# Four one-bank accumulators for a depthwise convolution, and its first two tiles of the larger group ahead of the first layer norm

## The chip, the core and the metric

The kernel runs on one core of a Trainium2 chip. Its engines are called PE (TensorE, matrix products; PEld is the loading of weights into it), DVE (VectorE), ACT (ScalarE), POOL (GpSimd) and SP (SyncE, which issues most DMAs here). Each engine works through its own queue in order and waits on semaphores for the others. The metric is the device time of one execution in microseconds (us).

## The reference, cut to what matters

One step of a streaming encoder, for one new stream of 512 frames and 8 running streams of 16 new frames each, D = 1024. Layer 0 is a convolution module and a feed-forward network (FFN); layer 1 is attention in bands of chunks, and an FFN. The change lies in layer 0's convolution module:

```python
def conv_module(h, hist, g, w_pw1, b_pw1, w_dw, b_dw, ln_g, ln_b, w_pw2, b_pw2):
    a, gate = jnp.split(rms_norm(h, g) @ w_pw1 + b_pw1, 2, axis=-1)
    glu = a * jax.nn.sigmoid(gate)
    full = jnp.concatenate([hist.astype(glu.dtype), glu], axis=1)
    y = lax.conv_general_dilated(
        full, w_dw[:, None, :].astype(full.dtype), window_strides=(1,), padding="VALID",
        dimension_numbers=("NWC", "WIO", "NWC"), feature_group_count=D_MODEL) + b_dw
    y = jax.nn.silu(layer_norm(y, ln_g, ln_b))
    return h + y @ w_pw2 + b_pw2, full[:, -CONV_HIST:]

def swiglu_ffn(h, g, w_in, w_out):
    a, b = jnp.split(rms_norm(h, g) @ w_in, 2, axis=-1)
    return h + (jax.nn.silu(a) * b) @ w_out
```

The depthwise convolution has 31 taps, so each of the 1024 channels is 31 multiply-adds along time. Everything is float32.

## The kernel before, in words

Features lie on the partitions, 8 channel tiles of 128, and the 640 frames on the columns, in two groups. The small group (g = 0) has 256 columns: the 128 frames of the running streams and the first 128 of the prompt. The larger group (g = 1) has the other 384 columns of the prompt.

A float32 product is made of three matmuls (`mm3`, L170 to L172): high part of the weight times high part of the data, low times high, high times low. So each weight is split after its load (`wsplit`, L128): ACT copies it to the high part (L150), and the low part is raw minus high (L154), of which DVE does the first columns and POOL the rest. For the FFN chunks of the small group, DVE does 512 of 2048 columns and POOL 1536 (384 and 1152 of 1536 for the output weights). A matmul of L171 needs the low part, so PE waits there for the slower of the two.

The steps of layer 0:

- pw1 and GLU, one channel tile at a time: products on PE, tanh and bias on ACT (L380, L383), the product of the two halves on DVE (L386 into `gs` for the small group, L395 into `gp` for the larger).
- the convolution, in three ways by channel tile. On DVE (`conv`, L420): per tap a multiply-add into an accumulator in PSUM (L434 the first tap, L437 the other 30), several tiles interleaved tap by tap; at the end ACT copies the sum to `y` (L440). On PE (`conv_pe`, with its staging through DRAM). On ACT and POOL (`conv_pool`): ACT multiplies, POOL adds into `y` (L417).
- the layer norm over the channels (`conv_ln`): POOL adds tiles of `y` (L195), PE sums over the partitions (L204), DVE collects (L208), PE spreads the mean (L216), DVE subtracts (L483); ACT squares (L179), POOL adds, PE sums, DVE and POOL make the root (L226, L230), DVE multiplies (L489), ACT applies the swish, and the result is split into high and low parts.
- pw2 (`pw2`), whose results DVE adds to `h` (L506), then the FFN. Its hidden tiles are worked in chunks of six. The first three chunks are done for the small group alone (chunk one, two and three here), each with six input weights and four output weights (output sums: L303); PE does them while DVE, ACT and POOL convolve for the larger group. Then pw2 of the larger group follows, and the other chunks for both groups.

The order in which the program is written out is the string `PLAN`, one token a step: `a`, `b` pw1 and GLU of a tile for the small and the larger group; `d` the convolution on DVE of one group (first digit) for the listed tiles, so `d0213` is the small group's tiles 2, 1 and 3, and `d101`, `d145`, `d127` are the larger group's tiles 0 and 1, 4 and 5, 2 and 7; `l` and `p` load and run the convolution on PE; `q` is the one on ACT and POOL; `n` the layer norm, `w` pw2, `r` the norm ahead of the FFN, `f` one chunk of the FFN, `s` the store of the convolution's history. A scheduler then orders each engine's queue by its own model of times, with higher priority for the weight splits and the GLU; the pools of buffers limit what can run ahead.

The accumulators come from the PSUM pool `w2`, which also serves the norms:

```python
w2 = w2s.enter_context(tc.tile_pool(name="w2", bufs=2, space=PSUM))
...
sts = [w2t() for _ in range(0, len(cs), 2)]
sts = [sts[i // 2][:, i % 2 * 512:i % 2 * 512 + n] for i in range(len(cs))]
```

It has two buffers of 1024 columns, that is two banks each. Two channel tiles share a buffer, one bank each.

## Time and profile before

| | |
|---|---|
| median of 3 runs | 1550.37 us (1547.32 to 1551.12) |
| the profiled run | 1551.3 us, of which the span is 1549.5 |
| instructions in the span | 26569 |
| mean granted PE clock | 0.984 |
| PE busy | 1471.7 us, 95% |
| DVE busy | 1050.1 us, 68% |
| ACT, POOL busy | 662.4 us (43%), 443.8 us (29%) |

The profile is of one execution. Its page gives the busy time of each engine over the span and over 40 equal slices (each digit is the busy share in tenths), and groups of instructions by source line: engine, operation, output and inputs by the program's names, shape, count, then busy time and the mean ns of one, then the idle time ahead of them. A timeline row gives start, duration, the instruction, and in brackets how long the engine had been idle and what ended that.

### The profile page before, as it was taken

What the parts mean: (1) busy time and instruction counts of PE and PEld (TensorE: products, weight loads), DVE (VectorE), ACT (ScalarE), POOL (GpSimd) and SP (SyncE); (2) the same over time, 40 slices, a digit from 0 to 9 for tenths busy, and PEclk for the clock granted to TensorE, in tenths of its full rate; (3) what the DMA queues carried; (4) which work ended last, traced back from release to release, by engine and by line L of the source; (5) the groups of instructions that cost most, each with busy time, mean ns of one, the idle gap of its engine ahead of it and who ended that gap; (6) DMA issues with size and microseconds to landing.
All of it is one profiled execution on the core that took longest, in us unless ns stands there. A gap on an engine that the chain in (4) does not pass through costs nothing.

```text
span 1549.5 us, 26569 instructions
## 1 busy us (share of the span) xinstructions
PE 1471.7 (95%) x10770; PEld 1398.9 (90%) x10770; DVE 1050.1 (68%) x1863; ACT 662.4 (43%) x1173; POOL 443.8 (29%) x403
## 2 busy tenths in 40 slices
PE   5888998989999999999999999999989999999997
PEld 5878888989999999999988798886989999999997
DVE  6994999988555455457576767566796476476455
ACT  4544454535423323235454445443554244244244
POOL 6865568877501000001321211110411121121110
PEclk9999999999999999999999999998999999999998
DMA  7784434444421333433655545453103213213211
GB/s 236 234 228 142 137 113 159 148 157 153 147 82 55 129 116 129 135 118 126 202 183 201 174 140 205 133 175 114 55 28 109 82 56 109 82 55 109 82 55 68
DMA packets 59658, 199.95 MB, mean 129 GB/s; under 512 B 10128, under 2 KB 22672, under 8 KB 46736
## 3 DMA queue, kind: packets, MB, share of 16 engines
q1 hardware_dynamic: 59248, 197.96, 39.1%
q8 instruction: 84, 1.38, 0.4%
q10 hardware_dynamic: 288, 0.31, 0.1%
q14 instruction: 38, 0.31, 0.1%
HBM read 187.02 MB, written 11.22 MB: 128 GB/s over the span
## 4 chain that ended last, share of the span: by engine, by line
PE 71%; DVE 16%; ACT 3%; issue 3%; DMA 3%; POOL 2%; SPq 0%; POOLq 0%; DVEq 0%; ACTq 0%
PE mm L170 12%; PE mm L172 12%; PE mm L171 12%; PE pb L968 6%; DVE w L437 5%; DVE wlo L154 4%; PE pc L968 4%; PE pa L968 4%; PE pb L170 1%; PE pb L171 1%; PE pb L172 1%; PE pa L172 1%; PE pa L170 1%; PE pc L170 1%; PE pc L172 1%
## 5 line engine op out<-in xcount | busy, mean ns | idle before, releaser
L171 PE MATMUL mm<-x,wlo 128*128 128x256 f32 (+1 forms) x1344 | 416.8, 312 | 15.4 <-DVE wlo L154 14.9
L170 PE MATMUL mm<-x,whi 128*128 128x256 f32 (+1 forms) x1344 | 413.3, 312 | 6.4 <-ACT x L159 3.7
L172 PE MATMUL mm<-x,whi 128*128 128x256 f32 (+1 forms) x1344 | 412.7, 311 | 0.5
L150 ACT ACTIVATE whi<-raw 128x2048 fp32r<-128x2048 f32 (+2 forms) x117 | 197.7, 1694 | 232.6 <-PE mm L172 138.8
L171 PEld LDWEIGHTS mm<-x,wlo 128*128 128x128 f32 x1344 | 257.1, 192 | 18.7 <-DVE wlo L154 17.5
L170 PEld LDWEIGHTS mm<-x,whi 128*128 128x128 f32 x1344 | 254.5, 191 | 11.2 <-ACT x L159 4.1
L172 PEld LDWEIGHTS mm<-x,whi 128*128 128x128 f32 x1344 | 255.1, 191 | 2.9 <-DVE x L160 1.8
L154 DVE TENSOR_TENSOR wlo<-raw,whi 128x2048 fp32r<-128x2048 f32 (+5 forms) x117 | 214.0, 1832 | 62.2 <-ACT whi L150 61.2
L154 POOL TENSOR_TENSOR wlo<-raw,whi 128x1536 fp32r<-128x1536 f32 (+3 forms) x50 | 145.7, 2918 | 69.0 <-ACT whi L150 69.0
L913 POOL TENSOR_TENSOR raw<-raw 128x512 f32<-128x512 f32 x38 | 50.5, 1330 | 332.3 <-DVE raw L913 257.5
L171 PE MATMUL mm<-hid,wlo 128*128 128x256 f32 (+1 forms) x352 | 107.7, 308 | 6.6 <-DVE wlo L154 6.6
L172 PE MATMUL mm<-hid,whi 128*128 128x256 f32 (+1 forms) x352 | 105.8, 307 | 0.2
L170 PE MATMUL mm<-hid,whi 128*128 128x256 f32 (+1 forms) x352 | 104.6, 307 | 0.1
L437 DVE SCALAR_TENSOR_TENSOR w<-gp,dwv,w 128x384 f32<-128x384 f32 x180 | 103.9, 612 | 0.8
L195 POOL TENSOR_TENSOR acc<-sq,sq 128x384 f32<-128x384 f32 (+1 forms) x8 | 8.1, 1006 | 258.2 <-ACT sq L179 258.1
L171 PEld LDWEIGHTS mm<-hid,wlo 128*128 128x128 f32 x352 | 66.0, 188 | 7.8 <-DVE wlo L154 7.8
L417 POOL TENSOR_TENSOR y<-y,cvt 128x256 f32<-128x256 f32 (+1 forms) x60 | 69.3, 1154 | 6.3 <-ACT cvt L416 4.0
L172 PEld LDWEIGHTS mm<-hid,whi 128*128 128x128 f32 x352 | 65.7, 188 | 0.6 <-DVE hid L160 0.6
L159 ACT ACTIVATE whi<-raw 128x1024 fp32r<-128x1024 f32 x38 | 39.4, 1054 | 61.6 <-PE pc L172 18.1
L170 PEld LDWEIGHTS mm<-hid,whi 128*128 128x128 f32 x352 | 65.2, 188 | 0.4 <-ACT hid L159 0.3
L968 PE MATMUL pa<-x0f,whi 128*128 128x320 f32 x228 | 61.2, 316 | 2.5 <-DVE t L913 2.3
L195 POOL TENSOR_TENSOR acc<-acc,sq 128x384 f32<-128x384 f32 (+1 forms) x48 | 52.7, 1097 | 28.9 <-ACT sq L179 27.5
(317 smaller groups left out, 3391.4 us busy)
## 6 DMA issues: line engine op xcount, KB each, us to landing
raw<-in_w_in SPq DMA_DIRECT2D x62, 1024.0 KB
raw<-in_w_out SPq DMA_DIRECT2D x36, 768.0 KB
raw<-in_w_pw SPq DMA_DIRECT2D x22, 1024.0 KB
cache<-in_ck SPq DMA_DIRECT2D x32, 512.0 KB
cache<-in_cv SPq DMA_DIRECT2D x32, 512.0 KB
raw<-in_w_kq SPq DMA_DIRECT2D x8, 1024.0 KB
x<-sc SPq DMA_DIRECT2D x16, 368.0 KB
raw<-in_w_out SPq DMA_DIRECT2D x4, 1024.0 KB
```

The source lines that it names most:

```text
L150: nc.scalar.activation(out=hi[:, a:b], in_=raw[:, a:b], func=AF.Copy)
L154: eng.tensor_tensor(out=lo[:, a:b], in0=raw[:, a:b], in1=hi[:, a:b].bitcast(F32), op=ALU.subtract)
L159: nc.scalar.activation(out=hi, in_=src, func=AF.Copy)
L170: nc.tensor.matmul(ps, wh, xh, start=(i == 0), stop=False)
L171: nc.tensor.matmul(ps, wl, xh, start=False, stop=False)
L172: nc.tensor.matmul(ps, wh, xl, start=False, stop=(i == last))
L195: last["acc"] = eng.tensor_tensor(out=acc[:, :n], in0=prev, in1=s(), op=ALU.add)
L417: nc.gpsimd.tensor_tensor(out=y[g][:, c, :], in0=y[g][:, c, :], in1=pr[:, :n], op=ALU.add)
L437: nc.vector.scalar_tensor_tensor(out=dst, in0=src, scalar=wj, in1=dst, op0=ALU.mult, op1=ALU.add)
L913: ENG[e].tensor_tensor(out=out, in0=a, in1=b, op=op)
L968: nc.tensor.matmul(ps, a[:, c], b[:, k, :], start=(first and k == 0 and i == 0), stop=(k == 3 and i == 2), skip_group_check=not first)
```

## The change

Four things, which belong together:

- The pool `w2` has four buffers of 512 columns (one bank) instead of two of 1024, and each channel tile of a convolution on DVE has a buffer of its own. The norm's sums move from column 512 to column 384 of their buffer, into the same bank as the spread mean. Before the attention the pool is closed and one of two buffers of 1024 columns opened, as the attention had it before.
- A convolution's first instructions are issued only behind the last instruction of the convolution ahead of it (`after(last.get("conv"))`).
- In `PLAN`, `d101` moves from behind `q16 s1` to just ahead of `n0`, the small group's layer norm.
- The layer norm `conv_ln` is written with high priority.

```diff
-PLAN = ("a0 y a1 a2 a4 x a3 a5 a6 l04 p04 l05 d0213 a7 b0 p05 b1 l07 p07 l06 b2 q00 s0 p06 n0 b3 b4 b5 d145 l13 w0 b7 r0 p13 b6 f q16 s1 d101 d127 n1 f f w1 r1")
+PLAN = ("a0 y a1 a2 a4 x a3 a5 a6 l04 p04 l05 d0213 a7 b0 p05 b1 l07 p07 l06 b2 q00 s0 p06 d101 n0 b3 b4 b5 d145 l13 w0 b7 r0 p13 b6 f q16 s1 d127 n1 f f w1 r1")
...
-    w2 = w2s.enter_context(tc.tile_pool(name="w2", bufs=2, space=PSUM))
+    w2 = w2s.enter_context(tc.tile_pool(name="w2", bufs=4, space=PSUM))
...
-    sums = [512]
+    wide_w2 = [512]
...
-        return w2.tile([P, 1024 if sums[0] == 512 else 512], F32, tag="w2", name=nm("w2"))
+        return w2.tile([P, wide_w2[0]], F32, tag="w2", name=nm("w2"))
...
+    def after(ins):
+        return tc.issue_after(ins.ins) if ins is not None else ExitStack()
...
-        w, c0 = len(srcs), sums[0]
+        w, c0 = len(srcs), 384
...
-        sts = [w2t() for _ in range(0, len(cs), 2)]
-        sts = [sts[i // 2][:, i % 2 * 512:i % 2 * 512 + n] for i in range(len(cs))]
+        sts = [w2t()[:, 0:n] for _ in cs]
...
                 if j == 0:
-                    nc.vector.tensor_scalar(out=dst, in0=src, scalar1=wj, scalar2=col(V_BDW, c),
-                                            op0=ALU.mult, op1=ALU.add)
+                    with after(last.get("conv")):
+                        nc.vector.tensor_scalar(out=dst, in0=src, scalar1=wj,
+                                                scalar2=col(V_BDW, c), op0=ALU.mult,
+                                                op1=ALU.add)
...
+        last["conv"] = end
...
-            zs[g] = conv_ln(g)
+            with tc.high_priority(offset=HP):
+                zs[g] = conv_ln(g)
...
+    w2s.close()
...
+    w2 = aps.enter_context(tc.tile_pool(name="w2a", bufs=2, space=PSUM))
+    wide_w2[0] = 1024
```

What this does to the queues, at three places. The rows are instructions in the order of one engine's queue: line, operation, output, inputs, shape, and a count where one repeats. The lines of the changed kernel stand 3 to 5 further down from the middle of the file on (L437 is L441, L483 is L488, L303 is L306).

First, DVE's queue in the small group's layer norm, before: from the sum's collection (L208) to the root (L226). `gp` is the GLU of the larger group, `wlo` a low part of a weight, `y` the convolved tile, `w_213` an accumulator.

```order
L208 TENSOR_REDUCE mst_1357<-w_168_1345 128x2
L480 COPY mst_1357<-mst_1357 128x2
L154 TENSOR_TENSOR wlo_1569<-raw_1567,whi_1568 128x2048
L483 TENSOR_TENSOR y_106<-y_106,w_168_1345 128x256 x8
L395 SCALAR_TENSOR_TENSOR gp<-t_204_1562,t_205_1564 128x384
L154 TENSOR_TENSOR wlo_1704<-raw_1702,whi_1703 128x1024
L434 TENSOR_SCALAR w_213_1628<-gp,dwv,vec 128x384
L226 TENSOR_SCALAR rst_1397<-w_171_1370 128x2
```

The same place after; `w_169` and `w_170` are the accumulators of `d101`.

```order
L211 TENSOR_REDUCE mst_1424<-w_171_1412 128x2
L441 SCALAR_TENSOR_TENSOR w_170_1347<-gp,dwv,w_170_1347 128x384
L441 SCALAR_TENSOR_TENSOR w_169_1346<-gp,dwv,w_169_1346 128x384
L485 COPY mst_1424<-mst_1424 128x2
L441 SCALAR_TENSOR_TENSOR w_170_1347<-gp,dwv,w_170_1347 128x384
L398 SCALAR_TENSOR_TENSOR gp<-t_200_1568,t_201_1570 128x384
L441 SCALAR_TENSOR_TENSOR w_169_1346<-gp,dwv,w_169_1346 128x384
L441 SCALAR_TENSOR_TENSOR w_170_1347<-gp,dwv,w_170_1347 128x384
L154 TENSOR_TENSOR wlo_1636<-raw_1634,whi_1635 128x2048
```

All 62 instructions of `d101` now stand between the small group's convolution and the norm's later steps; before, all of them stood behind that norm.

Second, DVE's queue at the end of chunk one. Before, the convolution (`w_366`, `w_367`, tiles of `d127` and `d101`) goes on past the last weight split of chunk one (`wlo_2683`), and past the first of chunk two:

```order
L154 TENSOR_TENSOR wlo_2683<-raw_2681,whi_2682 128x384
L437 SCALAR_TENSOR_TENSOR w_366_2820<-gp,dwv,w_366_2820 128x384
L437 SCALAR_TENSOR_TENSOR w_367_2885<-gp,dwv,w_367_2885 128x384
L303 TENSOR_TENSOR h<-mm_2641,h 128x256
L437 SCALAR_TENSOR_TENSOR w_366_2820<-gp,dwv,w_366_2820 128x384
```

After, the last split of chunk one is `wlo_2751`, and the first of chunk two `wlo_3061`:

```order
L154 TENSOR_TENSOR wlo_2751<-raw_2749,whi_2750 128x384
L441 SCALAR_TENSOR_TENSOR w_371_2889<-gp,dwv,w_371_2889 128x384
L441 SCALAR_TENSOR_TENSOR w_370_2888<-gp,dwv,w_370_2888 128x384
L306 TENSOR_TENSOR h<-mm_2709,h 128x256
L441 SCALAR_TENSOR_TENSOR w_371_2889<-gp,dwv,w_371_2889 128x384
L441 SCALAR_TENSOR_TENSOR w_370_2888<-gp,dwv,w_370_2888 128x384
L306 TENSOR_TENSOR h<-mm_2729,h 128x256
L441 SCALAR_TENSOR_TENSOR w_371_2889<-gp,dwv,w_371_2889 128x384
L441 SCALAR_TENSOR_TENSOR w_370_2888<-gp,dwv,w_370_2888 128x384
L441 SCALAR_TENSOR_TENSOR w_371_2889<-gp,dwv,w_371_2889 128x384
L306 TENSOR_TENSOR h<-mm_2756,h 128x256
L154 TENSOR_TENSOR wlo_3061<-raw_3059,whi_3060 128x512
```

Seven instructions of the convolution are left behind the last split of chunk one, and none behind the first of chunk two. Before, 78 were left at the same point.

Third, POOL's queue in chunk two after the change: the weight parts (`wlo`) and the adds of the tile that is convolved on ACT and POOL (L420, L417 before).

```order
L154 TENSOR_TENSOR wlo_3061<-raw_3059,whi_3060 128x1536
L420 TENSOR_TENSOR y_107<-y_107,cvt_2854 128x384
L154 TENSOR_TENSOR wlo_3124<-raw_3122,whi_3123 128x1536
L420 TENSOR_TENSOR y_107<-y_107,cvt_2857 128x384
L420 TENSOR_TENSOR y_107<-y_107,cvt_2860 128x384
L154 TENSOR_TENSOR wlo_3187<-raw_3185,whi_3186 128x1536
L420 TENSOR_TENSOR y_107<-y_107,cvt_2863 128x384
L420 TENSOR_TENSOR y_107<-y_107,cvt_2866 128x384
L154 TENSOR_TENSOR wlo_3250<-raw_3248,whi_3249 128x1536
```

Eleven of the 30 adds stand in chunk two, one or two behind each weight part; before, 15 did.

9 lines of the change are left out of this document (3 added, 6 removed).

## The prediction

> **What bounds the kernel now.** I read the page first: shares, then the slices, then the group of the convolution; after it the windows by stage, the waits, and the timelines of DVE and PE.
>
> ```profile
> span 1549.5 us, 26569 instructions
> PE 1471.7 (95%) x10770; PEld 1398.9 (90%) x10770; DVE 1050.1 (68%) x1863; ACT 662.4 (43%) x1173; POOL 443.8 (29%) x403
> DVE  6994999988555455457576767566796476476455
> L437 DVE SCALAR_TENSOR_TENSOR w<-gp,dwv,w 128x384 f32<-128x384 f32 x180 | 103.9, 612 | 0.8
> ```
>
> PE is busy 95% of the span, so the average says PE. But each slice is 38.7 us, and in slices 2 to 9 DVE is almost full, except the fourth. The convolution of the larger group on DVE (180 multiply-adds, 103.9 us of busy time) lies there. The next view cuts that region into stages; its columns are length, then busy time and instructions of PE, PEld, DVE, ACT and POOL, the granted clock, DMA share and GB/s.
>
> ```profile
> 120.09:151.67 31.58, 30.17 (x208) 28.79 (x200) 12.52 (x19) 13.17 (x22) 17.51 (x17) 1.00 0.43 135
> 151.67:169.82 18.15, 13.74 (x98) 13.25 (x98) 17.97 (x36) 12.66 (x21) 5.67 (x3) 0.81 0.17 59
> 169.82:260.16 90.34, 83.52 (x657) 77.80 (x658) 89.88 (x146) 42.40 (x62) 63.81 (x35) 0.98 0.44 140
> 264.43:331.59 67.16, 56.13 (x445) 54.08 (x444) 66.98 (x105) 30.82 (x38) 57.26 (x29) 0.96 0.45 144
> 331.59:388.18 56.59, 53.77 (x453) 53.17 (x453) 45.04 (x52) 28.15 (x39) 42.69 (x21) 0.99 0.49 165
> ```
>
> In 120 to 152 us, the first half of the first layer norm, PE works and DVE is idle for 31.58 - 12.52 = 19.1 us. From 152 to 331.6 DVE has no gap (17.97 of 18.15, 89.88 of 90.34, 66.98 of 67.16) and PE has. After the convolution PE is the fuller one. What PE waits for between 264 and 388 us:
>
> ```profile
> PE mm L171 <- DVE wlo L154: 13.2, 10, 3.6
> PE mm L170 <- ACT whi L150: 0.4, 1, 0.4
> ```
>
> Nearly all of it is for DVE's part of a weight split, which stands in DVE's queue behind convolution instructions. So the region is one chain: DVE up to the end of the convolution, PE behind it. The next rows are its marks (start, duration, engine, and in brackets the wait ahead): the end of the small group's convolution at 120.09, the two long waits of the norm, the last weight split of the first FFN chunk, the last convolution instructions; then on PE the starts of chunks two and three and of pw2 of the larger group.
>
> ```profile
> 118.61 0.56 DVE L395 SCALAR_TENSOR_TENSOR gp<-t,t 128x384 f32<-128x384 f32 x1 [1.18 <-ACT t L380]
> 119.08 1.01 DVE L437 SCALAR_TENSOR_TENSOR w<-gs,dwv,w 128x256 f32<-128x256 f32 x2
> 131.58 0.56 DVE L395 SCALAR_TENSOR_TENSOR gp<-t,t 128x384 f32<-128x384 f32 x1 [8.87 <-ACT t L380]
> 149.59 0.16 DVE L226 TENSOR_SCALAR rst<-w 128x2 f32<-128x2 f32 x1 [4.70 <-PE w L204]
> 258.15 2.09 DVE L154 TENSOR_TENSOR wlo<-raw,whi 128x384 fp32r<-128x384 f32 x1
> 330.42 1.26 DVE L437 SCALAR_TENSOR_TENSOR w<-gp,dwv,w 128x384 f32<-128x384 f32 x2
> 264.43 0.39 PE L170 MATMUL mm<-x,whi 128*128 128x256 f32 x2
> 325.63 0.50 PE L170 MATMUL mm<-x,whi 128*128 128x256 f32 x2 [0.41 <-ACT whi L150]
> 388.18 0.51 PE L170 MATMUL mm<-x,whi 128*128 128x384 f32 x2
> ```
>
> The last weight split of chunk one ends about 260.2, and PE ends the chunk 4.2 us behind it, at 264.4. Chunks two and three take 388.18 - 264.43 = 123.75 us. From pw2 of the larger group on, the instructions and their order are the same before and after, up to one swap of two SP transfers, so the end moves by what 388.18 moves.
>
> **The change, part by part.**
>
> *DVE's stretch from 120.09 to the last split of chunk one.* Busy time of before: 12.52 + 17.97 + 89.88 = 120.4 us. Before, 108 of the larger group's 186 convolution instructions stand in it, and 78 behind it; after, by the order, 179 and 7. So 71 more have to pass before the last split. Their price is a pitch, not a duration, because neighbours overlap:
>
> ```profile
> 162.58 2.59 DVE L437 SCALAR_TENSOR_TENSOR w<-gp,dwv,w 128x384 f32<-128x384 f32 x4
> 272.55 3.23 DVE L437 SCALAR_TENSOR_TENSOR w<-gp,dwv,w 128x384 f32<-128x384 f32 x6
> ```
>
> The first four all add into one buffer, each to what the one before it wrote: (2.59 - 0.612)/3 = 0.66 us from start to start. The six alternate between two buffers: (3.23 - 0.612)/5 = 0.52 us. After, the tiles alternate throughout: 71 x 0.525 = +37.3 us. Of before's 108, 18 follow directly on one of their own buffer, and none does after: 18 x 0.13 = -2.4 us. This is the whole gain of the four one-bank buffers on DVE. Work of the stretch after: 120.4 + 37.3 - 2.4 = 155.3 us.
>
> [...]
>
> Start: the wait of 1.18 us ahead of the product at 118.61 is filled, since the moved convolution's first two instructions stand ahead of that product now; the stretch starts at 120.09 - 1.18 = 118.9. Idle: the 8.87 and 4.70 us above are now filled with the moved tiles (62 instructions, 32 us, stand between the norm's steps). What stays are short waits for PE's spread of a mean, of which before shows these:
>
> ```profile
> 137.01 2.74 DVE L483 TENSOR_TENSOR y<-y,w 128x256 f32<-128x256 f32 x8 [1.34 <-PE w L216]
> 151.67 1.42 DVE L489 TENSOR_TENSOR y<-y,w 128x256 f32<-128x256 f32 x4 [0.65 <-PE w L216]
> ```
>
> I take 3.5 us: these 2.0, and 1.5 for the norm's last square on ACT and last accumulation on POOL, which stand behind one more weight step than before. The bounds are 0 and the 19.1 of before. Last split of chunk one: 118.9 + 155.3 + 3.5 = 277.7, and PE's end of the chunk 277.7 + 4.3 = 282.0, which is 17.6 us later than 264.4. What PE loses ahead of that (the first layer norm's end comes later, as does pw2 of the small group) costs nothing: PE was idle for 12.6 us in the first three windows (31.58 - 30.17, 18.15 - 13.74, 90.34 - 83.52), and DVE's queue, 17.5 us longer, adds as much. If DVE were not full, this cover would be gone.
>
> *Chunks two and three.* DVE has lost all but 7 of 78 convolution instructions here, so PE sets the pace, unless POOL does. PE's pace and POOL's instructions in chunk two (the second view is groups between 265 and 326 us: count, busy, mean ns):
>
> ```profile
> 293.50:298.50 5.00, 5.00 (x44) 5.00 (x44) 5.00 (x10) 2.65 (x5) 4.92 (x3) 1.00 0.50 161
> L154 POOL TENSOR_TENSOR wlo<-raw,whi 128x1536 fp32r<-128x1536 f32 x7 | 24.4, 3490 | 6.7 <-ACT whi L150 6.7
> L417 POOL TENSOR_TENSOR y<-y,cvt 128x384 f32<-128x384 f32 x15 | 18.9, 1257 | 0.5
> L154 POOL TENSOR_TENSOR wlo<-raw,whi 128x1152 fp32r<-128x1152 f32 x4 | 10.7, 2670 | 3.9 <-ACT whi L150 3.9
> ```
>
> A chunk for the small group is 432 matmuls (six hidden tiles of 48, eight outputs of 18), 5.00/44 = 0.1136 us each: 49.1 us. Three things come on top in chunk two:
> - Its first split on DVE stands behind the convolution's end and a residual add. In before the same spot cost 2.68 and 3.56 us (rows below). I take 1.7, since 7 instructions are left and not a stream; bounds 0 and 3.6.
> - POOL still has 11 adds of the tile that it convolves; the order sets one or two of them behind each weight part. A weight with two: 3.49 + 2 x 1.257 = 6.0 us on POOL against 48 x 0.1136 = 5.45 on PE, so 0.55 us for five weights, 2.7 us. In the outputs two accumulations of the larger norm (1.17 each) stand between weights: 2.67 + 2.34 = 5.0 against 36 x 0.1136 = 4.1, once: 1.0 us. Bounds 0 (POOL ran ahead far enough) and 6.
> - The larger norm's steps on ACT and DVE go beside this, since DVE is no longer full.
>
> ```profile
> 267.49 0.38 PE L171 MATMUL mm<-x,wlo 128*128 128x256 f32 x1 [2.68 <-DVE wlo L154]
> 329.69 0.58 PE L171 MATMUL mm<-x,wlo 128*128 128x256 f32 x1 [3.56 <-DVE wlo L154]
> 353.30 3.49 POOL L154 TENSOR_TENSOR wlo<-raw,whi 128x1536 fp32r<-128x1536 f32 x1 [0.79 <-ACT whi L150]
> 353.90 3.44 DVE L154 TENSOR_TENSOR wlo<-raw,whi 128x512 fp32r<-128x512 f32 x1
> ```
>
> Chunk two: 49.1 + 1.7 + 3.7 = 54.5 us. Chunk three has been free of the convolution in before too, from 331.59: 56.59 us for 453 matmuls, the norm's 30 small ones among them. It takes 9 more of the chunk's matmuls (1.0 us) and does not have the lower clock behind the wait at 329.69 (0.8 us): 56.8. Together 111.3 us against 123.75. Bounds: 2 x 49.1 + 3.8 for the norm's small matmuls = 102 below, 116 above (the two bounds of chunk two added).
>
> *Moved without cost:* pw2 of the larger group starts when chunk three ends, with its norm done, as in before. In the order, one SP transfer (a convolution tile's staging store) stands behind one more weight load; its tile is convolved on PE inside the stretch where PE has time. Closing and reopening the pool before attention moves no instruction there.
>
> *Sum.* 282.0 + 111.3 = 393.3, against 388.18: +5.1 us. The profiled run took 1551.3 us (span 1549.5, 1.8 outside), 0.9 above the median of the runs. So 1556.4 by the profiled run, 1555.5 by the median. The convolution ends 50 us sooner, but what was pushed ahead of the splits of chunk one comes back as PE's wait there, and chunks two and three give back less than that.
>
> **Rivals.**
>
> B: chunks two and three run at PE's pace. POOL's adds are done ahead of the splits; then they take 111.3 - 3.7 - 1.5 = 106.1, and the time is 1550.3. For it: POOL is only 17.51 of 31.58 us busy in the norm's stretch, where ACT may feed it earlier. Against: POOL is 57.26 of 67.16 busy in chunk two of before, and 63.81 of 90.34 in chunk one, with splits that come first. It decides when fewer than five adds are left as chunk two starts.
>
> C, the other side: DVE's splits get shorter. The splits on DVE in chunk one, and in the last row the same kind from 388 to 422 us:
>
> ```profile
> L154 DVE TENSOR_TENSOR wlo<-raw,whi 128x512 fp32r<-128x512 f32 x6 | 11.9, 1985 | 0.0
> L154 DVE TENSOR_TENSOR wlo<-raw,whi 128x1024 fp32r<-128x1024 f32 x3 | 7.3, 2418 | 0.0
> L154 DVE TENSOR_TENSOR wlo<-raw,whi 128x1024 fp32r<-128x1024 f32 x3 | 3.8, 1279 | 3.4 <-ACT whi L150 3.4
> ```
>
> At half the width of the last row's a split would take 0.64 us (an estimate from the 1279 ns). So six splits carry 6 x 1.35 and three 3 x 1.14 us, 11.5 in all, in which DVE's instruction lasts as long as POOL's beside it; the row at 353.90 above shows one that ends with POOL's. If the later DVE finds POOL done when it reaches a split, 10 of these go: chunk one ends at 272 and the time is 1545.5. Against: POOL has the same splits and adds in a stretch only a fifth longer. It decides when most splits start behind POOL's.
>
> D: DVE waits for the norm after all. Its queue is in order; where a norm's step comes before the filling instructions are used up, DVE stands still. The norm's chain leads through ACT, POOL and PE, and one more weight step stands ahead of its last square and last accumulation. With 13 us idle instead of 3.5: 1565. For it: in before the chain lasted to 149.6 although DVE was idle and free to serve it. Against: 32 us of filling for 13.6 us of waits.
>
> [...]
>
> **How the numbers follow.** About 0.3% (4.65 us) is what a measurement of this kernel can tell from no change: faster below 1545.7, slower above 1555.0. Forecast 0.43, and as its bounds (idle, start stall, POOL) lie on both sides of 1555.0, slower 0.27 and same 0.16. B 0.22: same 0.17, faster 0.05. C 0.16: faster 0.13, same 0.03. D 0.14 and E 0.05: slower. Faster 0.18, same 0.36, slower 0.46. The range, 1544 to 1566, reaches from C's time to D's and leaves out 0.2; the forecast's own is 1550 to 1561.
>
> **What would show it.** Right: DVE without a gap from about 135 to 280 us; last split of chunk one at about 278 and its end on PE near 282; PE's waits for DVE's splits grown to about 30 us ahead of that; chunk two in about 54 us with POOL's weight parts the last to arrive; pw2 of the larger group at about 393. Wrong, if DVE idles for more than 8 us between 119 and 160 (D), if the splits of chunk one average under 1.2 us at 512 columns (C), if PE's matmuls of chunk two show no wait for POOL (B), or if anything behind pw2 of the larger group moves.

## The result: 1570.5 us against 1550.2, and where the 20 us lie

The changed kernel takes 1570.49 us (median of 4 runs, 1568.45 to 1576.18), the kernel before 1550.22 beside it (1547.32 to 1551.12). The ratio is 1.014, with a 95% interval from 1.011 to 1.0169: slower, by four times the forecast's +5 and outside its range. The profiled run took 1570.38 us.

The page of the changed kernel, with the lines that answer to those shown of before:

```profile
span 1568.6 us, 26572 instructions
PE 1478.1 (94%) x10770; PEld 1403.2 (89%) x10770; DVE 1067.7 (68%) x1863; ACT 662.7 (42%) x1173; POOL 442.7 (28%) x403
L441 DVE SCALAR_TENSOR_TENSOR w<-gp,dwv,w 128x384 f32<-128x384 f32 x180 | 100.3, 612 | 0.0
```

The totals alone explain nothing: PE has the same matmuls, and DVE is 17.6 us busier although the convolution's group is 3.6 us shorter. So the other instructions of DVE got longer (their number is the same). The windows by stage (columns as in the prediction): the first half of the first norm, the rest of it, from there to the convolution's last instructions, then the three chunks.

```profile
119.39:152.00 32.61, 30.43 (x220) 28.82 (x220) 29.82 (x53) 13.47 (x19) 14.36 (x12) 1.00 0.46 148
152.00:169.80 17.80, 8.24 (x44) 7.56 (x45) 17.80 (x35) 6.62 (x14) 4.71 (x3) 0.62 0.17 60
169.80:283.69 113.89, 97.37 (x721) 90.29 (x721) 112.06 (x184) 51.68 (x77) 69.49 (x40) 0.93 0.35 111
218.10:287.95 69.85, 57.26 (x433) 55.22 (x433) 68.02 (x111) 35.41 (x51) 53.28 (x30) 0.90 0.39 122
287.95:346.15 58.20, 53.13 (x453) 52.14 (x451) 43.99 (x38) 27.85 (x36) 53.38 (x27) 1.00 0.49 164
346.15:406.94 60.79, 55.89 (x447) 54.56 (x445) 50.35 (x53) 32.55 (x45) 42.97 (x19) 0.94 0.47 157
```

The first row is as forecast: DVE's 19.1 idle microseconds are filled, 29.82 of 32.61. The second already isn't: PE has 8.24 us of work in 17.80, where before it had 13.74 in 18.15, and its granted clock is 0.62 instead of 0.81. The marks on PE (pw2 of the small group, the three chunks, pw2 of the larger group) and on DVE (the last weight split of chunk one):

```profile
163.60 0.58 PE L170 MATMUL mm<-x,whi 128*128 128x256 f32 x1 [2.37 <-ACT x L159]
...
218.10 0.28 PE L170 MATMUL mm<-x,whi 128*128 128x256 f32 x1
...
287.95 0.39 PE L170 MATMUL mm<-x,whi 128*128 128x256 f32 x2
...
346.15 0.28 PE L170 MATMUL mm<-x,whi 128*128 128x256 f32 x1
...
406.94 0.51 PE L170 MATMUL mm<-x,whi 128*128 128x384 f32 x2
...
281.67 2.09 DVE L154 TENSOR_TENSOR wlo<-raw,whi 128x384 fp32r<-128x384 f32 x1
```

The larger pw2 starts at 406.94 instead of 388.18, 18.8 us later, which is the loss within the difference of two single profiles (the spans differ by 19.1). It is made of four pieces: pw2 of the small group starts 9.3 us later (154.28 before), it and the products of the larger group behind it take 4.4 more (chunk one starts at 218.10, before at 204.34), chunk one takes 69.85 us instead of 60.09, and chunks two and three give back only 4.8 (58.20 and 60.79 together, 123.75 before).

**The first norm.** Four queues show the 9.3 us: ACT, POOL, DVE and PE of the changed kernel, then ACT's, POOL's and PE's rows for the same sums in the kernel before.

```profile
152.35 0.40 ACT L182 ACTIVATE sq<-y 128x256 f32<-128x256 f32 x1
...
152.53 2.34 POOL L154 TENSOR_TENSOR wlo<-raw,whi 128x1024 fp32r<-128x1024 f32 x1 [1.19 <-ACT whi L150]
154.82 1.71 POOL L198 TENSOR_TENSOR acc<-acc,sq 128x256 f32<-128x256 f32 x1
...
152.72 3.23 DVE L154 TENSOR_TENSOR wlo<-raw,whi 128x1024 fp32r<-128x1024 f32 x1
155.87 3.24 DVE L441 SCALAR_TENSOR_TENSOR w<-gp,dwv,w 128x384 f32<-128x384 f32 x6
159.02 0.15 DVE L229 TENSOR_SCALAR rst<-w 128x2 f32<-128x2 f32 x1
...
156.59 1.02 PE L207 MATMUL w<-onec,acc 128*128 128x1 f32 x4 [6.71 <-POOL acc L198]
```

```profile
147.29 0.42 ACT L179 ACTIVATE sq<-y 128x256 f32<-128x256 f32 x1 [1.81 <-POOL acc L195]
...
146.52 2.37 POOL L195 TENSOR_TENSOR acc<-acc,sq 128x256 f32<-128x256 f32 x3
...
148.94 0.61 PE L204 MATMUL w<-onec,acc 128*128 128x1 f32 x4
```

In the changed kernel one more weight stands in the norm's way: ACT copies its high part (150.56 to 152.46) ahead of the norm's last square, which starts at 152.35 instead of 147.29, and POOL makes its low part ahead of the last accumulation (154.82), which ends at 156.5 instead of 148.9. That is 7.6 us. PE sums at once (until 157.6), but DVE has six convolution instructions of 3.24 us queued ahead of the root's first step, and reaches it at 159.02, not 149.59: 1.4 us more. PE meanwhile has run out of other work.

**Chunk one.** Its inputs come from the FFN norm of the small group: eight times a product `n` (L243, now L246) and a low part `x` (L160) on DVE. DVE's timeline around the start of chunk one, before (at 204.34) and after (at 218.10):

```profile
202.02 0.87 DVE L243 SCALAR_TENSOR_TENSOR n<-h,vec,w 128x256 f32<-128x256 f32 x2
202.81 0.62 DVE L437 SCALAR_TENSOR_TENSOR w<-gp,dwv,w 128x384 f32<-128x384 f32 x1
203.33 0.76 DVE L160 TENSOR_TENSOR x<-n,x 128x256 fp32r<-128x256 f32 x2
...
205.83 0.68 DVE L434 TENSOR_SCALAR w<-gp,dwv,vec 128x384 f32<-128x384 f32 x1
206.42 0.75 DVE L160 TENSOR_TENSOR x<-n,x 128x256 fp32r<-128x256 f32 x2
```

```profile
218.18 0.42 DVE L160 TENSOR_TENSOR x<-n,x 128x256 fp32r<-128x256 f32 x1
218.51 0.48 DVE L246 SCALAR_TENSOR_TENSOR n<-h,vec,w 128x256 f32<-128x256 f32 x1
218.90 1.14 DVE L441 SCALAR_TENSOR_TENSOR w<-gp,dwv,w 128x384 f32<-128x384 f32 x2
219.95 0.48 DVE L246 SCALAR_TENSOR_TENSOR n<-h,vec,w 128x256 f32<-128x256 f32 x1
...
230.03 0.41 DVE L160 TENSOR_TENSOR x<-n,x 128x256 fp32r<-128x256 f32 x1
```

Before, norm steps come in pairs with one convolution instruction between; the last two `x` start 2.1 and 2.4 us behind the start of chunk one (the pair at 206.42). After, they mostly come singly with two convolution instructions between; the last `x` is at 230.03, 11.9 us behind. From the first `n` to the end of the last `x` the steps take 10.2 us with 9 convolution instructions between them before, and 19.0 us with 19 after.

What chunk one loses on PE shows in its window of before (the changed kernel's is above, 218.10 on) and in PE's waits in the chunk, before and after:

```profile
204.34:264.43 60.09, 53.40 (x434) 51.48 (x433) 60.09 (x101) 32.94 (x45) 48.83 (x26) 0.97 0.46 142
```

```profile
PE mm L171 <- DVE wlo L154: 6.5, 7, 2.1
```

```profile
PE mm L171 <- DVE wlo L154: 11.0, 6, 3.6
```

PE scarcely waits for an `x` itself. It waits 4.5 us more for weight splits, which stand behind these steps in DVE's queue, 1.3 us for a copy on ACT, and its matmuls keep it busy 3.9 us longer (57.26 against 53.40), at a granted clock of 0.90 instead of 0.97. Together these are the 9.8 us.

### The profile page after: what moved, and what is told of

Read it like the earlier page. It is cut to its first block, busy times and chain, and to the rows that moved or that the text cites. A ratio compares the mean times of both kernels' runs of the same rounds, so it can differ in the third digit from the quotient of the medians.

```text
span 1568.6 us, 26572 instructions
## 1 busy us (share of the span) xinstructions
PE 1478.1 (94%) x10770; PEld 1403.2 (89%) x10770; DVE 1067.7 (68%) x1863; ACT 662.7 (42%) x1173; POOL 442.7 (28%) x403
## 4 chain that ended last, share of the span: by engine, by line
PE 74%; DVE 14%; ACT 3%; issue 3%; DMA 3%; POOL 2%; SPq 0%; POOLq 0%; DVEq 0%; ACTq 0%
PE mm L170 14%; PE mm L171 14%; PE mm L172 14%; PE pb L973 6%; DVE w L441 4%; PE pc L973 4%; PE pa L973 4%; DVE wlo L154 3%; ACT whi L150 2%; PE pb L170 1%; PE pb L171 1%; PE pb L172 1%; PE pa L172 1%; PE pa L170 1%; PE pc L170 1%
## 5 line engine op out<-in xcount | busy, mean ns | idle before, releaser
L170 PE MATMUL mm<-x,whi 128*128 128x256 f32 (+1 forms) x1344 | 414.2, 313 | 10.2 <-ACT whi L150 5.3
L154 DVE TENSOR_TENSOR wlo<-raw,whi 128x2048 fp32r<-128x2048 f32 (+5 forms) x117 | 228.5, 1955 | 67.6 <-ACT whi L150 63.9
L172 PE MATMUL mm<-hid,whi 128*128 128x256 f32 (+1 forms) x352 | 107.4, 311 | 0.8 <-DVE hid L160 0.8
L170 PE MATMUL mm<-hid,whi 128*128 128x256 f32 (+1 forms) x352 | 106.2, 311 | 1.8 <-DVE h L306 1.5
L441 DVE SCALAR_TENSOR_TENSOR w<-gp,dwv,w 128x384 f32<-128x384 f32 x180 | 100.3, 612 | 0.0
L420 POOL TENSOR_TENSOR y<-y,cvt 128x256 f32<-128x256 f32 (+1 forms) x60 | 66.7, 1112 | 7.2 <-ACT cvt L419 4.9
L159 ACT ACTIVATE whi<-raw 128x1024 fp32r<-128x1024 f32 x38 | 39.5, 1055 | 60.6 <-PE pc L172 18.1
L973 PE MATMUL pa<-x0f,whi 128*128 128x320 f32 x228 | 60.1, 311 | 2.4 <-DVE t L918 2.3
```

The source lines that it names most:

```text
L154: eng.tensor_tensor(out=lo[:, a:b], in0=raw[:, a:b], in1=hi[:, a:b].bitcast(F32), op=ALU.subtract)
L159: nc.scalar.activation(out=hi, in_=src, func=AF.Copy)
L170: nc.tensor.matmul(ps, wh, xh, start=(i == 0), stop=False)
L172: nc.tensor.matmul(ps, wh, xl, start=False, stop=(i == last))
L420: nc.gpsimd.tensor_tensor(out=y[g][:, c, :], in0=y[g][:, c, :], in1=pr[:, :n], op=ALU.add)
L441: end = nc.vector.scalar_tensor_tensor(out=dst, in0=src, scalar=wj, in1=dst, op0=ALU.mult, op1=ALU.add)
```

## The experiments

The chunks are compared by the starts of their first matmuls on PE. "n to x" is the time from the first `n` to the last `x` of the small FFN norm on DVE, with the number of convolution instructions between. Lengths are of one profile each; where two kernels had the same work in a chunk they differed by 1 to 2 us. Medians are of 4 runs or more, ratios are to the kernel before on the same chip, with 95% intervals.

| kernel | pw2 small | one starts | one | two | three | pw2 larger | n to x | median | ratio |
|---|---|---|---|---|---|---|---|---|---|
| before | 154.3 | 204.3 | 60.1 | 61.2 | 62.6 | 388.2 | 10.2, 9 | 1550.22 | |
| changed | 163.6 | 218.1 | 69.8 | 58.2 | 60.8 | 406.9 | 19.0, 19 | 1570.49 | 1.014 [1.011, 1.0169] |
| buffers | 156.3 | 213.3 | 72.6 | 59.7 | 62.4 | 408.0 | 19.3, 18 | 1573.91 | 1.0149 [1.0101, 1.0196] |
| buffers_noafter | 157.1 | 216.0 | 75.0 | 65.1 | 57.4 | 413.5 | 23.4, 24 | 1574.52 | 1.0145 [1.0125, 1.0165] |
| before_after | 151.4 | 201.1 | 59.2 | 61.9 | 73.4 | 395.7 | 9.6, 8 | 1559.36 | 1.0059 [1.0036, 1.0081] |
| c1pool | 163.3 | 219.0 | 72.1 | 55.7 | 57.4 | 404.2 | 21.4, 21 | 1571.25 | 1.0136 [1.0096, 1.0175] |
| c23even | 162.2 | 217.8 | 68.2 | 57.1 | 57.5 | 400.6 | 19.0, 19 | 1566.84 | 1.0107 [1.0067, 1.0148] |
| d127late | 166.4 | 221.8 | 66.0 | 60.6 | 64.4 | 412.7 | 19.0, 19 | 1572.6 | 1.0142 [1.0101, 1.0183] |
| alldve | 163.5 | 218.8 | 71.3 | 60.4 | 52.5 | 402.9 | 20.2, 19 | 1564.91 | 1.0092 [1.0065, 1.0119] |
| noq | 165.0 | 220.8 | 66.6 | 61.5 | 56.1 | 405.0 | 18.2, 19 | 1565.72 | 1.0098 [1.007, 1.0127] |
| split_dve | 163.1 | 218.8 | 68.6 | 52.7 | 56.5 | 396.7 | 20.2, 19 | 1560.12 | 1.0051 [1.0029, 1.0073] |
| buf_late | 158.0 | 208.0 | 72.4 | 59.8 | 62.8 | 402.9 | 19.2, 17 | 1563.46 | 1.0073 [1.0048, 1.0098] |
| d10_p3 | 154.7 | 204.4 | 73.0 | 59.1 | 61.4 | 398.0 | 23.6, 23 | 1559.65 | 1.0063 [1.0043, 1.0083] |
| before_c3dve | 153.7 | 203.1 | 60.5 | 60.3 | 62.0 | 385.9 | 10.2, 9 | 1550.17 | 0.9995 [0.9986, 1.0003] |
| gate | 165.7 | 221.0 | 57.8 | 57.9 | 60.3 | 397.0 | 7.2, 1 | 1562.7 | 1.0081 [1.0052, 1.011] |
| gate2 | 157.2 | 208.4 | 60.6 | 61.2 | 58.5 | 388.8 | 6.9, 1 | 1551.57 | 1.0008 [0.9993, 1.0024] |
| gate2_c3 | 153.6 | 205.9 | 60.2 | 60.6 | 57.4 | 384.1 | 6.9, 1 | 1549.43 | 0.9995 [0.9979, 1.0012] |
| gate2_c23 | 157.0 | 208.9 | 60.4 | 59.1 | 59.1 | 387.5 | 6.9, 1 | 1549.88 | 0.9997 [0.9982, 1.0013] |
| gate2_p2 | 157.7 | 210.2 | 57.0 | 61.2 | 57.0 | 385.5 | 6.9, 1 | 1546.01 | 0.9967 [0.9953, 0.9982] |

### Which part of the change

`buffers` is the changed kernel with the old order and priority, so the buffers and the serial issue remain:

```diff
-PLAN = ("... q00 s0 p06 d101 n0 b3 ... q16 s1 d127 n1 ...")
+PLAN = ("... q00 s0 p06 n0 b3 ... q16 s1 d101 d127 n1 ...")
-            with tc.high_priority(offset=HP):
-                zs[g] = conv_ln(g)
+            zs[g] = conv_ln(g)
```

> Four one-bank buffers, each convolution behind the last, no move of d101 in PLAN, no high priority for the norm. By its order 48 instructions of the convolution stand behind the last weight split of chunk one (before 78, after 7). Theory Q (DVE's queue up to that split sets the end of chunk one, at about 0.525 us for each convolution instruction ahead of it): the 19 us of idle DVE in the first norm stay, 30 x 0.525 - 2.4 = 13 us more work than before, so chunk one ends at about 277; chunks two and three take 112 to 118 us; pw2 of the larger group starts at 389 to 395, 1551 to 1557 us. Rival N (the moved tile holds up the first norm and pw2 of the small group, and PE's gap at 152 to 170 us is the loss): no such hold-up here, chunk one ends near 265 and the time is 1540 to 1548 us.

It is as slow as the changed kernel, and its chunk one longer: 72.6 us. So the 20 us do not need the move in the order and the priority; only their place differs (pw2 of the small group starts 2.0 us later than before, not 9.3, and takes 33.3 us instead of 26.5; in the changed kernel it takes 29.6). Two further kernels split what is left. `buffers_noafter` has the four buffers without the serial issue; `before_after` has the serial issue alone, with the two pairs of banks of before:

```diff
 buffers_noafter, against buffers
-                    with after(last.get("conv")):
+                    with ExitStack():
 before_after, against before
+                    with (tc.issue_after(last["conv"].ins) if "conv" in last else ExitStack()):
                         nc.vector.tensor_scalar(out=dst, in0=src, scalar1=wj, ...)
```

> The kernel of run buffers without the serial issue: only the four one-bank buffers remain of the change. Theory N: the order puts two to four convolution instructions between the splits of the first norm's result as in buffers, so pw2 of the small group again takes 31 to 34 us, chunk one starts near 213 and lasts 68 us or more; 1565 to 1575 us. Rival S (the serial issue is what costs): chunk one starts by 207 and lasts near 60 us, 1548 to 1556 us.

> The kernel before, with only one part of the change: a convolution's first instructions are issued behind the last instruction of the convolution ahead of it (the two-bank buffers, PLAN and the norm's priority are those of before). Up to the end of pw2 of the small group its queues are before's. Theory N (the start of chunk one decides, and the chunks are about as long whatever the convolution's place): chunk one starts at 204 and ends by 268; the larger norm's inputs come later in the order, so chunk three or pw2 of the larger group may wait: 1550 to 1562 us. Rival S (the serial issue is what costs): chunk one lasts 66 us or more as in buffers, 1565 us or above.

The four buffers alone give the whole loss, with chunk one at 75.0 us. The serial issue alone leaves chunk one at 59.2, and costs its 9 us elsewhere: the convolution ends at 348.7 us instead of 331.7, well into chunk three, which lasts 73.4 us with the larger norm behind it.

### Is it the splits that DVE and POOL share?

My first theory of chunk one was the split of each weight between DVE and POOL. These kernels change POOL's share of it in quarters, by chunk, or free one of the engines:

```diff
-            ffn({0: hp0}, w_in0, w_out0, {0: late[0]}, (0,), (chunks.pop(0),), PFA)
+            ffn({0: hp0}, w_in0, w_out0, {0: late[0]}, (0,), (chunks.pop(0),), {2: A, 1: B, 0: C}[len(chunks)])
```

The changed kernel has A, B, C = 3, 3, 3; `c1pool` has 4, 3, 3, `c23even` 3, 2, 2, `alldve` 0, 0, 0, and `before_c3dve` is the kernel before with 3, 3, 0.

> The changed kernel, with the weight splits of chunk one wholly on POOL. Theory Q: DVE loses 20.6 us of splits ahead of the end of chunk one, which then comes at 268 to 274 instead of 288, held by POOL (about 4.7 us a weight and the adds); some of it is given back in chunk two, where more of POOL's adds are left: 1554 to 1562 us. Rival N: chunk one is held by its late start behind the norm and by PE, not by DVE's queue: it ends within 3 us of 288, or later, 1569 to 1576 us.

> The changed kernel, with the weight splits of chunks two and three half on DVE and half on POOL (before a quarter and three quarters). Theory P (in chunks two and three POOL's queue sets the pace, 6.2 us for a weight part of 1536 columns and two adds against 5.45 us of matmuls, and DVE's splits last until POOL's instruction ends): chunk two 58.2 to about 52 us, chunk three 60.8 to about 57: 1558 to 1563 us. Rival D (DVE's own steps of the larger norm between the splits set it): DVE gets more work and chunks two and three stay at 119 us or grow, 1569 to 1575 us.

> The changed kernel, with the weight splits of chunks one to three wholly on DVE, none on POOL. Theory L (DVE's split, both of whose inputs lie in SBUF, lasts until POOL's instruction beside it ends, so the weights come at POOL's pace, about 6.2 us each with the adds, whatever DVE does): a whole split takes DVE 2.3 us, less than the 2.6 to 4 us that a quarter takes beside POOL; chunk one stays near 70 us (DVE full of the convolution), chunks two and three take 52 to 55 us each instead of 58.2 and 60.8: 1556 to 1562 us. Rival Q (DVE's queue is the bound and POOL's share relieves it): chunk one grows by 5 us or more and the time is 1570 us or above.

> The kernel before, with the weight splits of chunk three wholly on DVE (before a quarter on DVE and three quarters on POOL); no convolution is left on DVE there but its first 3 us. Theory L (a split on DVE lasts until POOL's instruction beside it ends; without POOL a whole split takes 2.3 us): chunk three 62.6 to 55-59 us, 1543 to 1547 us, faster than both kernels. Rival Q (DVE gets 15 us more work beside the larger norm's steps and holds PE): chunk three 63 us or more, 1550 to 1555 us.

`c1pool` takes DVE's splits out of chunk one, and chunk one isn't shorter (72.1). `c23even` gains 4.3 us in chunks two and three together. `alldve` comes nearest to PE's pace, in a chunk three with no convolution, two last steps of the norm and next to nothing on POOL, against the 49.1 us of matmuls:

```profile
350.50:402.90 52.40, 51.05 (x434) 50.64 (x433) 28.79 (x34) 21.63 (x23) 1.22 (x1) 1.00 0.52 181
```

Its chunk two, with the larger norm inside, still takes 60.4. In the kernel before, the same edit in chunk three gains nothing that can be told (62.0 us, ratio 0.9995): there the larger norm lies in it.

`noq` leaves out 30 of the 31 taps of the larger group's tile on ACT and POOL, so POOL's adds and ACT's products for them are gone from the chunks:

```diff
-        for j in range(W):
+        for j in range(W if g == 0 else 1):
```

> The changed kernel without 30 of the 31 taps of the larger group's tile that is convolved on ACT and POOL (only the first tap is left), so POOL has none of those adds and ACT none of the products in chunks one and two. Theory L: POOL's weight parts come without adds between them, chunk one 69.8 to 62-66 us, chunk two 58.2 to 52-54 us: 1552 to 1561 us. Rival Q: DVE's queue is as long as before, chunk one ends within 3 us of 288; only chunk two could gain: 1565 to 1571 us.

Chunk two is 3.3 us longer (61.5), chunk one 3.3 us shorter and chunk three 4.7. The forecast's term for POOL's adds in chunk two is not seen as such.

### Is it the number of convolution instructions ahead of the splits?

This was the forecast's own premise. `d127late` issues the last two tiles only behind the last output sum of chunk one (`last["h"]`), so that DVE has 12 multiply-adds in chunk one where the changed kernel has 72:

```diff
+            last["h"] = nc.vector.tensor_tensor(out=hp(g, m), ...)
-                    with after(last.get("conv")):
+                    with after(last["h"] if cs == [2, 7] else last.get("conv")):
```

> The changed kernel, with the last two convolution tiles (d127) issued on DVE only behind the last output sum of chunk one: 62 instructions behind the last split of chunk one instead of 7. Theory Q: chunk one ends 55 x 0.525 = 29 us sooner unless PE holds it before, at 260 to 266; chunks two and three carry 32 us more of DVE's work and take 126 to 134 us: pw2 of the larger group at 388 to 398, 1550 to 1560 us. Rival N: chunk one ends later than 278, 1565 us or more.

Chunk one ends at the same time, 287.7. It started 3.7 us later, so it is 3.9 us shorter, where 60 instructions at 0.52 us would be 31. Its window and DVE's groups in it:

```profile
221.80:287.70 65.90, 54.02 (x433) 52.63 (x432) 50.90 (x51) 35.05 (x50) 52.31 (x29) 0.95 0.41 130
```

```profile
L154 DVE TENSOR_TENSOR wlo<-raw,whi 128x512 fp32r<-128x512 f32 x6 | 19.6, 3271 | 3.3 <-ACT whi L150 3.3
L154 DVE TENSOR_TENSOR wlo<-raw,whi 128x384 fp32r<-128x384 f32 x4 | 10.2, 2556 | 1.8 <-POOL y L421 1.6 <-ACT whi L150 0.2
```

DVE is idle for 15 us of the 65.9, and yet the splits are longer: 3271 ns against 2571 in the changed kernel's chunk one, the 384-column ones 2556 against 1208. So the number of convolution instructions in front does not price a chunk. Much of what DVE gains by having less to do goes into idle time and into splits that last until POOL's part is done (see the last section). `split_dve` puts both together: no share for POOL, and of the last two tiles one in chunk one and one behind it (`PLAN` with `d12 d17`, the second issued behind `last["h"]`).

> As alldve, and of d127 the second tile is issued only behind the last output sum of chunk one, so that DVE's work is spread more evenly over chunks one and two. Theory L: chunk one about 60 us, chunk two 54, chunk three 53, pw2 of the larger group near 386: 1546 to 1552 us. Rival Q: chunk one shorter by 16 us and chunk two longer by as much: 1568 to 1573 us.

At 1560.12 it is 10 us better than the changed kernel, in chunk two (52.7) and three (56.5); chunk one stays at 68.6, and the start of chunk one at 218.8. Those two pieces no share of POOL's had moved by more than 3 us.

### Is it the convolution between the norm's steps?

`buf_late` is `buffers` with the first instructions of `d145` held behind the last `x` of the small group's convolution norm; `d10_p3` has tile 0 alone ahead of that norm and tiles 1, 4 and 5 held behind it (`d10 n0 ... d1145`):

```diff
 buf_late (last["x"] is the last low part issued; d10_p3 has cs == [1, 4, 5])
-                    with after(last.get("conv")):
+                    with after(last["x"] if cs == [4, 5] else last.get("conv")):
```

> The kernel of run buffers (four one-bank buffers, no move of d101), with the second convolution d145 issued only behind the first norm's last split of its result, so that none of its instructions stands between those splits. Theory N (PE's path is held at pw2 of the small group, because convolution instructions stand in DVE's queue between the norm's splits, and this delay is never won back): pw2 of the small group takes 25 to 27 us instead of 33.2, chunk one starts near 206, and the time is 1546 to 1554 us. Rival Q (only the number of convolution instructions ahead of the last split of chunk one counts, about 22 fewer here than in buffers, 12 us): 1559 to 1564 us.

> The changed kernel, but only one tile (channel tile 0) is convolved ahead of the first norm; tile 1 goes with tiles 4 and 5, which are issued only behind the last split of that norm's result; the norm has no high priority. Theory N: the 31 instructions (16 to 20 us) fit into DVE's idle 19 us and hold nothing up, pw2 of the small group starts at 154 to 158 and takes 25 to 27 us, chunk one starts at 205 to 209; chunks one to three take 185 to 192 us: 1554 to 1563 us. Rival Q (DVE's count ahead of the last split): about 24 more than before, 12 us less idle, chunk one ends near 275, as late as in buffers or later: 1565 us or above.

Both bring back the start of chunk one: `buf_late` from the 213.3 of `buffers` to 208.0, and `d10_p3` to 204.4, that of before within 0.1 us. In `buf_late` the whole gain reaches the larger pw2, 5.1 us sooner than in `buffers`. Neither shortens chunk one, 72.4 and 73.0 us: there 17 and 23 convolution instructions lie in the FFN norm. So the late start and the long chunk one are two losses. In `buffers` the first is convolution between the norm's steps, like the second. In the changed kernel most of it is the weight ahead of the norm's last sum on ACT and POOL; `d10_p3` is free of it, but it leaves out both the second tile ahead of the norm and the norm's priority, and no run tells which of the two brings it. `gate` takes the second loss alone from the changed kernel: `d145` is written behind `r0`, the small FFN norm, and held behind its last `x`.

```diff
-PLAN = ("... d101 n0 b3 b4 b5 d145 l13 w0 b7 r0 p13 ...")
+PLAN = ("... d101 n0 b3 b4 b5 l13 w0 b7 r0 d145 p13 ...")
-                    with after(last.get("conv")):
+                    with after(last["x"] if cs[0] in (4,) else last.get("conv")):
```

> The changed kernel, with the convolution d145 moved in PLAN behind r0 and its first instructions issued only behind the last split of the FFN's input (the norm r0), so that none stands between that norm's steps. Theory X (chunk one is long because convolution instructions stand between the steps of the norm whose result its first weights need; in before the second buffer was held by that norm, and only one convolution ran): chunk one starts at 213 to 218, the last split of its input ends within 4 us of that instead of 12.3, and chunk one lasts 59 to 62 us instead of 69.8; chunks two and three, with more convolution in them, 121 to 126: pw2 of the larger group near 398, 1558 to 1565 us. Rival Q (DVE's queue up to the last split): DVE loses some 15 us to idling before chunk one, and about as much conv work stands in chunk one, so chunk one lasts as long as before, and the time is 1570 us or above.

Chunk one falls from 69.85 to 57.8 us, with the late start unmended (221.0). DVE's timeline of `gate` around the norm:

```profile
212.66 0.86 DVE L247 SCALAR_TENSOR_TENSOR n<-h,vec,w 128x256 f32<-128x256 f32 x2
...
219.47 0.43 DVE L160 TENSOR_TENSOR x<-n,x 128x256 fp32r<-128x256 f32 x1 [0.35 <-ACT x L159]
```

All steps are done 1.1 us ahead of the chunk. The windows of the chunk's first 16.8 us, of the changed kernel and of `gate`, show what that is worth to PE: 88 matmuls against 131, at a granted clock of 0.80 against 1.00.

```profile
218.10:234.90 16.80, 13.33 (x88) 12.92 (x88) 15.61 (x28) 7.83 (x14) 10.42 (x7) 0.80 0.27 71
```

```profile
221.00:237.80 16.80, 15.16 (x131) 14.77 (x130) 16.80 (x27) 10.05 (x13) 13.89 (x7) 1.00 0.45 123
```

The 43 matmuls are 4.9 us at 0.1136. In the whole chunk PE's waits for splits fall from 11.0 us to 4.9:

```profile
PE mm L172 <- DVE wlo L154: 4.9, 8, 1.7
```

Its busy time falls from 57.26 to 52.3 us for the same work, with the granted clock at 1.00 instead of 0.90. So about half of the gain is waits and not quite half is the clock; the runs do not tell whether the one follows from the other. The groups on DVE in the whole chunk one, of the changed kernel and of `gate`, show the same from DVE's side:

```profile
L441 DVE SCALAR_TENSOR_TENSOR w<-gp,dwv,w 128x384 f32<-128x384 f32 x72 | 40.5, 610 | 0.0
L154 DVE TENSOR_TENSOR wlo<-raw,whi 128x512 fp32r<-128x512 f32 x5 | 12.9, 2571 | 0.0
...
L160 DVE TENSOR_TENSOR x<-n,x 128x256 fp32r<-128x256 f32 x5 | 2.9, 576 | 0.0
...
L246 DVE SCALAR_TENSOR_TENSOR n<-h,vec,w 128x256 f32<-128x256 f32 x4 | 1.9, 475 | 0.0
```

```profile
L442 DVE SCALAR_TENSOR_TENSOR w<-gp,dwv,w 128x384 f32<-128x384 f32 x67 | 37.4, 610 | 0.0
L154 DVE TENSOR_TENSOR wlo<-raw,whi 128x512 fp32r<-128x512 f32 x5 | 8.5, 1708 | 0.0
```

DVE is full in this chunk in both kernels (68.02 of 69.85, 57.80 of 57.80). The changed kernel's has the norm's nine late steps in it (2.9 + 1.9 = 4.8 us), 4.4 us more in its five splits, four more convolution instructions in all (2.1 us at 0.52), and 1.8 us of idle time: 13.1 us, for the 12.05 between the two lengths.

`gate2` takes the first loss too: `d10` ahead of the convolution norm, `d11` held behind its last `x`, `d145` behind that of `r0`, no priority for the norm.

> As gate, but only one tile is convolved ahead of the first norm (channel tile 0), a second (tile 1) behind the last split of that norm's result, and d145 behind the FFN's norm; no high priority for the norm. Theory X: the first norm is not held up either: chunk one starts at 202 to 206, lasts 59 to 62 us, chunks two and three 120 to 125 us: pw2 of the larger group at 382 to 392, 1544 to 1554 us, about the kernel before or faster. Rival Q: 124 convolution instructions behind the start of chunk one against 147 in before: 12 us faster than before, 1536 to 1541 us. Rival B (one-bank accumulators are slower in themselves): chunk one 66 us or more, 1557 us or above.

Pw2 of the small group starts at 157.2, chunk one at 208.4 and lasts 60.6: 1551.57 us, ratio 1.0008. With four one-bank buffers, one tile ahead of the first norm instead of two, no priority for that norm, and the convolution kept out of two norms, the whole loss is gone. In this form the change is worth nothing that can be measured.

### Is there anything to gain beyond that?

On `gate2`, POOL's shares of the splits in chunks one to three, in quarters: `gate2_c3` 3, 3, 2; `gate2_c23` 3, 2, 2; `gate2_p2` 2, 2, 2.

> As gate2, with the splits of chunk three half on DVE and half on POOL. By run c23even (chunks two and three 119.0 to 114.7 us with half the split on DVE): chunk three 2 to 4 us shorter than in gate2. By run before_c3dve, where chunk three stayed at 62.0 us with the whole split on DVE: no difference beyond 1 us.

> As gate2, with the splits of chunks two and three half on DVE and half on POOL. Theory L (POOL's part and the adds behind it set the pace and hold DVE's): chunk two 61 to 57-59 us, chunk three 57 to 58: 1545 to 1549 us. Rival Q (DVE is full of convolution in chunk two): chunk two 62 us or more, 1550 to 1553 us.

> As gate2_c23, in chunk one too. Theory L: chunk one 60 to 57-59 us as well: 1543 to 1548 us, faster than both kernels. Rival Q: chunk one, where DVE has no gap, grows by the wider splits to 62 to 64 us: 1552 to 1556 us.

The first two are equal to before. `gate2_p2` beats both kernels: 1546.01 us (12 runs), ratio 0.9967 with an interval from 0.9953 to 0.9982, about 5 us. In its chunk one (57.0 us against 60.6 in `gate2`) PE's waits for DVE's splits are 2.1 us, and 7.9 in `gate2`. The kernel before with these shares was not run, so it is not shown that the 5 us need the four buffers.

## Why the prediction was wrong, step by step

The forecast's sum had pw2 of the larger group at 393.3; it came at 406.94, 13.6 us later. Of these, 5.9 lie in the end of chunk one (287.95 against 282.0) and 7.7 in chunks two and three (119.0 against 111.3).

- **"What PE loses ahead of that ... costs nothing".** This is the step that failed most. The forecast let chunk one end by DVE's queue alone (its last split at 277.7, PE's end at 282.0) and counted PE's lost time ahead of it as slack, to come back as about 30 us of waits for DVE's splits. From 119 us to the end of chunk one these waits are 11.7 us (8.3 before). PE lost its time elsewhere: 11.5 us in the three waits of the first norm (6.71, 2.41 and 2.37; before 4.0), 4.3 in waits for copies on ACT (before none), and from the start of the small pw2 to the end of chunk one 6.1 us of busy time for the same matmuls (107.6 against 101.5), at a granted clock of 0.92 instead of 0.96. The forecast put the clock at nothing here. The chunk starts 13.8 us later, and the steps `n` and `x` of its own norm, out of the same DVE queue, then stand ahead of its splits. Where these steps are freed the time follows: the larger pw2 comes 9.9 us sooner in `gate`, and at before's time, within 0.6 us, in `gate2`. Both also leave more convolution behind (121 and 123 instructions in the three chunks, 73 in the changed kernel), but `d127late` shows that leaving it behind gains nothing by itself.
- **The premise behind it: 71 more instructions "have to pass before the last split".** As a count it held: 179 and 7 were as the order said, and DVE's stretch was full (112.06 of 113.89). The last split ended at 283.8 instead of 277.7: the stretch began 0.5 us later than forecast (119.39), since the wait of 1.18 us that was to be filled came again as 1.77, DVE's busy time was 4.4 us over the sum, and its idle time 1.1 over the 3.5. PE's end came 4.2 us behind that split, as forecast, at 287.95 instead of 282.0. As a cause it fell: with 60 fewer convolution instructions inside the chunk (`d127late`) the chunk ended at 287.7.
- **"1.5 us for the norm's last square and accumulation".** The forecast named the place ("stand behind one more weight step than before"), and mis-sized it: the root's first step came 9.4 us later (159.02 against 149.59). 7.6 of it are that weight step, on ACT and on POOL, and 1.4 are convolution instructions ahead of the root. DVE did not idle for it, as the term assumed; it worked on convolution instructions while PE stood still. The price was on PE.
- **Chunks two and three: 54.5 + 56.8 = 111.3 us.** Measured 58.2 + 60.8 = 119.0. "PE sets the pace" did not come true: PE's waits in them add up to 9.9 us, 7.3 of them for DVE's splits:

```profile
PE mm L171 <- DVE wlo L154: 7.3, 6, 2.6
...
```

  And "the larger norm's steps go beside this" was wrong, by an estimate of 4 to 8 us: with all splits on DVE, `alldve` has nearly the whole norm in chunk two (60.4, eight convolution instructions with it) and only two of its steps in chunk three (52.5); `split_dve` has the norm's first half in chunk two (52.7) and the second in chunk three (56.5).
- **The -2.4 us of the four buffers.** The shorter pitch is there, with 13 instructions in a row 0.526 us apart, (6.92 - 0.612)/12, where before's chained ones took 0.66. No run shows it in the time.

```profile
123.40 6.92 DVE L441 SCALAR_TENSOR_TENSOR w<-gp,dwv,w 128x384 f32<-128x384 f32 x13
```

- **The rivals.** B (PE's pace in chunks two and three) did not happen. Nor did E, the chance of 0.05 for the forecast without its -2.4 us: alternating, the pitch was 0.526 us, against 0.66 on one buffer before. B's term of 1.5 us is not worked out in the forecast. C had the tie between DVE's splits and POOL's parts in its hands and gave it the wrong sign: the 512-column splits grew from 1985 to 2626 ns on average. D came nearest by its time, 1565, and named the late norm, but as idle time of DVE, of which the norm's stretch had 2.8 us (32.61 - 29.82); the wait was PE's.
- **What was missed altogether.** The buffers change what stands between a norm's steps. `buffers_noafter` and `before_after` show that they do it (24 convolution instructions between `n` and `x` with four buffers and nothing else, 8 with the old ones), and `gate` that keeping these instructions out gives chunk one its 12 us back. How the buffers do it is in part argued. In the kernel before, a norm's sums take one of the two, and the next convolution starts only behind the norm's last `n` (its first tap at 205.83, that `n` ends at 205.40); in `buffers` it starts ahead of the first `n` (206.6 and 207.8). In the changed kernel, though, only one convolution stands beside the FFN norm too, so the scheduler's setting 19 instructions where 9 were has a reason that no run shows.

What stays open: what sets the 57 to 61 us of a chunk with convolution beside it. Neither POOL's shares alone (`c1pool`, `gate2_c3`), nor POOL's adds (`noq`), nor the count on DVE (`d127late`) moves it to the 52.5 us that `alldve` has without them. Only `split_dve`, with no shares and a single tile on DVE, has such a chunk at 52.7; which of the two it takes was not separated. And of `gate2_p2`'s 5 us only chunks one and three show where they were gained, by amounts (3.6 and 1.5 us) of which the second is within what two profiles differ by. In the changed kernel's own late first norm, the second tile ahead of it and the norm's priority were not separated, and in chunk one the lower clock was not separated from the waits.

## What to carry to other kernels

A pool's few buffers can be what keeps filler work (instructions that are only there to use an idle engine) out of a latency chain; before adding buffers, look at what the freed queue will put between the steps of the next norm, and who waits for its result. Filling an engine's idle time is free only for that engine: follow the chain that passes through its queue to the consumer, and charge the consumer's wait. When a count of instructions explains the end of a stage, take them out once and see whether the end moves.
